# Eleven gate blocks placed anew in a hybrid DeltaNet and linear attention layer: one at the end of the linear attention, six in the delta rule, four behind it

## The chip, the cores and the metric

The kernel runs on one core of one Trainium2 chip. The metric is device microseconds of one execution. All numbers are in float32; matrix products that need the accuracy are made of three passes on TensorE with operands split into a high and a low part (type fp32r).

## The reference

One layer over a sequence of 1024 tokens of width 1024. What matters here are the two merge gates: two column groups of the one input projection, whose sigmoids weigh the two branches.

```python
h = rmsnorm(x, norm_mix_g[i])
proj = h @ w_in[i]
(gq, gk_, gv, gz, ga, gb, lq, lk, lv, lr, lgate, gate_a, gate_b) = jnp.split(proj, split_at, axis=-1)
...
o_a = gated_delta_rule_chunked(q_a, k_a, v_a, ...)        # 8 heads of 128, chunked
o_a = rmsnorm(o_a, gdn_norm_g[i]) * silu(gz)
y_a = o_a @ w_branch_gdn[i]
...
o_b = gla_chunked(q_b, k_b, v_b, ...)                     # 4 heads, linear attention
o_b = rmsnorm(o_b, gla_norm_g[i]) * silu(lr)
y_b = o_b @ w_branch_gla[i]

merged = jax.nn.sigmoid(gate_a) * y_a + jax.nn.sigmoid(gate_b) * y_b
x = x + merged @ w_out[i]
# then cross attention over 256 memory tokens, a squared-relu MLP, a final norm
```

gate_a and gate_b are 1024 columns each. Together they are 16 blocks of 128 columns, and each block needs only h (the normed input) and its own weights. A block may be computed at any time between the norm of x and the merge. That freedom is what the change uses.

## The kernel before, in words

**Phases in order.** Folding of the cross attention's weights and the norm of x; gate blocks 0 to 3; linear attention (`phase_gla`, 4 heads h, gate block 4 among its first projection); delta rule (`phase_gdn`, 4 pairs p of heads); two gate blocks and the loading of the merge's operands (in `run`); merge (`phase_merge`), output projection, cross attention and MLP.

**A gate block** (`push_gate`) is a unit of dense work: weights of 512 KB are loaded and split (ScalarE copies the high part, VectorE or GpSimd subtracts for the low part), 2 halves of 24 matmuls of 512 columns each follow into one PSUM tile each, ScalarE takes the tanh of each half into an SBUF tile, and SP stores it to DRAM (`tgd[i]`). The merge later loads these 32 halves back. The normed h stands in four slots of SBUF (A0a, A0b, A1a, A1b); every gate block and every projection of the delta rule reads them.

**Dense units and fills.** `push` puts a unit into a queue as a generator; each step of it emits one matmul (a unit of 48 matmuls has 49 steps, since one is spent after its weights). `fill(n)` takes n steps from the front of the queue, `until(name)` runs the queue to the end of a named unit, `drain` empties it. The phases are written as short chains (scan, norm, substitution) with such calls between their parts, so that TensorE has matmuls to do while a chain waits on VectorE or ScalarE.

**The delta rule's pair.** Per pair the queue gets q (2 units), v (2), a gate block, the next pair's keys (2), another gate block, z (2). The chain is: keys of the first head; output of the pair before (`gdn_norm`, then, once the queue has been run to its z, `gdn_out` with transposes and L1379, then `gdn_sums`, which stores to `oad`); keys of the second head; substitution (`gdn_subst`: 31 steps of two VectorE operations, L1250 and L1252); queries and v; inverse (`gdn_inverse`); scan over 8 chunks (`gdn_scan`). The fills between them come from GF and NFILL: 24 + 24 + 16 between the v units and the inverse, 8 four times in the inverse, 4 at 22 places in the scan. Behind the last pair one more gate block is pushed, 12 steps are filled, the norm is issued, 20 more are filled, and the outputs follow.

**The linear attention's end.** The last head (h = 3) has the unit r3 (84 matmuls, gate of the output) as its only dense work. Its scan has no fills (FI = 0); then `gla_norm` (L1045 scales the output v), the rest of the queue, and `gla_out` (transposes of v, L582, and the products that are stored to `obd`).

**Behind the delta rule.** `run` opens the SBUF pools of the merge in the memory that the delta rule leaves, pushes gate blocks 14 and 15, issues the loads of the operands of merge passes 0 to 3 (`obd` through three staging tiles "e", then splits into the slots B0a, B0b, B1a, B1b), and drains. Only then are passes 4 to 6 loaded, into t4 (memory of the gate blocks' weights), A1a and A1b (memory of h). The first merge product makes 7 passes in that order, for two groups of columns at once, 12 matmuls each.

**What sets the order.** The Python order is not the order of issue. The program is traced once, a planner (`Plan`) simulates it with costs of its own, and its order for every engine is laid down in a second trace. TensorE takes the matmul that stands earliest in the trace among those that are ready; the other engines go by latest start times. Tiles of one tag keep their order. So a change of the trace changes the planned order everywhere, within what is ready and what buffers allow. DMAs are issued by SP in the planned order, each waiting at the head of the queue.

Few lines that the words don't say, from `phase_gla`:

```python
                self.until(f"r{h}")
                self.gla_norm(sp, v[h % 2], ss)
```

for the first three heads, and for the last

```python
                    self.gla_norm(sp, v[h % 2], ss)
                    self.drain()
                    self.gla_out(sp, h, v[h % 2], sr)
```

Of the kernel before, what the change touches and what calls it, by code (L numbers as in the profile page):

```python
# [18 lines left out]
P = 128  # L19
D = 1024  # L20
T = 1024
NB = 8
MEM = 256
GH = 8
LH = 4
XH = 4
EPS = 1e-6
HALF = 512
# [13 lines left out]
XO = (('K3', 'Q1', 'V0'), ('V0', 'V1', 'O2'))  # L42
LOVU = (5,)
LOV = (0, 2, 5)


def c3(t):
# [393 lines left out]
class Layer:  # L441
# [624 lines left out]
    def phase_gla(self):  # L1066
        nc, a = self.nc, self.a
        with ExitStack() as ctx:
            sp = self.pool(ctx, "pgla", "right", bufs=2)
            self.bs[3] = self.late_h(self.t1d, lambda: self.ext(sp))  # L1070
            sm = self.sm = self.til(sp, [P, T], "sm", bufs=1)
            for tag, shape in (("qk", [P, T]), ("v", [P, NB, 256])):
                self.til(sp, shape, tag, bufs=2)
            self.pad(sp, 64)
            g4 = self.ext(sp)

            def done(i, half):
                if i == 1:
                    x = g4[:, half * HALF:(half + 1) * HALF]
                    nc.scalar.activation(x, x, AF.Tanh, scale=0.5)  # L1080
                    nc.sync.dma_start(self.tgd[4][:, half * HALF:(half + 1) * HALF], x)

            qk, ev = self.gla_qk(sp)
            self.push("u0", self.gla_dense([self.into(lambda i, half: (sm, g4)[i][:, half * HALF:(half + 1) * HALF],
                                                      1.0, done), ev]))
            self.until("u0")
            v = self.push_gla_v(sp, 0)
            self.fill(FA)
            bc = self.gla_gate(sp, 0)
            gb = self.decay_rows(sp)  # L1090
            prep = self.gla_prep(sp, qk, bc)
            self.until("v0")
            self.decay_cols(gb)
            sr = self.push_gla_r(sp, 0)
            self.fill(FB)
            for h in range(LH):
                AT, kdt = self.gla_scores(sp, *prep[:3], qk[1])
                self.fill(FC)
                ss = self.gla_scan(sp, AT, kdt, qk[0], v[h % 2], prep[3], FH if h < LH - 1 else FI)
                if h == LH - 1:  # L1100
# [3 lines that stand above are left out]
                    break  # L1104
                self.until(f"r{h}")
                self.gla_norm(sp, v[h % 2], ss)
                bc = self.gla_gate(sp, h + 1)
                qk, ev = self.gla_qk(sp)
                self.push(f"qk{h + 1}", self.gla_dense([ev]))
                self.fill(FD)  # L1110
                self.gla_out(sp, h, v[h % 2], sr)
                self.until(f"qk{h + 1}")
                prep = self.gla_prep(sp, qk, bc)
                if h == 1:
                    v = self.push_gla_v(sp, 2)
                    self.until("v2")
                    self.fill(FB)
                after = None
                if h == LH - 2:
                    def after(p):  # L1120
                        if p == 3:
                            self.hb[0, 1] = self.late_h(self.b12d, lambda: self.til(self.wp, [P, T], "raw", bufs=RAWS))
                sr = self.push_gla_r(sp, h + 1, after)
                self.fill(FG if h == 1 else FE)


# [266 lines left out]
        for q, x in enumerate((b11, b21, T2, T1, T3, b22, T4)):  # L1393
            nc.sync.dma_start(self.oad[q][:, p], x)

    def push_gate(self, i, getw, sp, tag="tg", tbufs=3):

        nc = self.nc

        def evict(half, pt):  # L1400
            t = self.til(sp, [P, HALF], tag, bufs=tbufs)
            nc.scalar.activation(t, pt, AF.Tanh, scale=0.5)
            nc.sync.dma_start(self.tgd[i][:, half * HALF:(half + 1) * HALF], t)

        self.push(f"g{i}", self.g_fm(lambda: getw(self.a["w_gate"][i]), evict))

    def phase_gdn(self, wp):

        nc, a = self.nc, self.a
        with ExitStack() as ctx:  # L1410
            sp = self.pool(ctx, "pgdn", "right", bufs=2)
            sq = self.pool(ctx, "pgdn2", "right", bufs=2)
            self.subPT = self.til(sp, [P, 16, P], "subPT", bufs=1)
            nc.gpsimd.memset(self.subPT, 0.0)
            self.pad(sp, 224, ([P, T], "k", 4), ([P, T], "dm", 2), ([P, T], "q", 2), ([P, T + 64], "cin", 2), ([P, T], "kdt", 2),
                     ([P, T], "NT", 2), ([P, T], "Pm", 1), ([P, 256], "pr", 1), ([P, 16, P], "PF", 1))

            for tag in ("v", "X", "acc", "AT"):
                self.til(sq, [P, T], tag, bufs=2)
            self.pad(sq, 96, ([P, HALF], "tg", 3))  # L1420

            def push_keys(hs):
                sts = [{}, {}]
                for h, st in zip(hs, sts):
                    st["k"] = self.til(sp, [P, NB, P], "k", bufs=4)
                    self.push_conv(wp, sp, sq, f"k{h}", GH + h, a["w_gdn"][4 * h], lambda acc, st=st: st["k"])
                return sts

            gates = iter(range(5, 14))
            getw = lambda src: self.wunit(wp, src)  # L1430
            last = None
            sts = push_keys((0, 1))
            for st, h in zip(sts, (0, 1)):
                self.gdn_decay(sp, sq, h, st)
            for p in range(GH // 2):
                hs = (2 * p, 2 * p + 1)
                for h, st in zip(hs, sts):
                    st["q"] = self.til(sp, [P, NB, P], "q", bufs=2)
                    self.push_conv(wp, sp, sq, f"q{h}", h, a["w_gdn"][4 * h + 1], lambda acc, st=st: st["q"])
                for h, st in zip(hs, sts):  # L1440
                    def out(acc, st=st):
                        st["vT"] = c3(acc)
                        return st["vT"]
                    self.push_conv(wp, sp, sq, f"v{h}", 2 * GH + h, a["w_gdn"][4 * h + 2], out)
                self.push_gate(next(gates), getw, sq)
                nxt = None
                if p < GH // 2 - 1:
                    nxt = push_keys((2 * p + 2, 2 * p + 3))
                self.push_gate(next(gates), getw, sq)
                for h, st in zip(hs, sts):  # L1450
                    self.push_gdn_z(wp, sp, sq, h, st)
                self.until(f"k{hs[1]}")
                self.fill(GF[0])
                if last:
                    for h, st in last:
                        self.gdn_norm(sq, st)
                self.gdn_keys(sp, sq, hs[0], sts[0])
                self.fill(GF[1])
                if last:
                    self.until(f"z{last[1][0]}")  # L1460
                    for h, st in last:
                        self.gdn_out(h, st)
                        self.fill(GF[2])
                    self.gdn_sums(p - 1, [st for _, st in last])
                self.gdn_keys(sp, sq, hs[1], sts[1])
                PF = self.gdn_subst(sp, sq, sts)
                self.until(f"v{hs[0]}")
                self.gdn_queries(sp, sq, sts[0])
                self.fill(GF[3])
                self.gdn_queries(sp, sq, sts[1])  # L1470
                self.until(f"v{hs[1]}")
                self.gdn_v(sq, sts[0])
                self.fill(GF[4])
                self.gdn_v(sq, sts[1])
                self.fill(GF[5])
                self.gdn_inverse(sts, PF, GF[6])
                if nxt:
                    for st, h in zip(nxt, (2 * p + 2, 2 * p + 3)):
                        self.gdn_decay(sp, sq, h, st)
                self.gdn_scan(sq, hs, sts, NFILL)  # L1480
                last, sts = list(zip(hs, sts)), nxt
            self.push_gate(next(gates), getw, sq)
            self.fill(12)
            for h, st in last:
                self.gdn_norm(sq, st)
            self.until(f"z{last[1][0]}")
            self.fill(20)
            for h, st in last:
                self.gdn_out(h, st)
            self.gdn_sums(3, [st for _, st in last])  # L1490
            self.drain()
# [691 lines left out]
    def run(self):  # L2183
# [41 lines left out]
        with ExitStack() as ctx:  # L2225
# [2 lines left out]
            sp = self.pool(self.ctx, "plate", "right")  # L2228
            self.pad(sp, 32, ([P, HALF], "e", 3), ([P, HALF], "acc", 2), ([P, HALF], "q", 4))
            self.bp2 = self.pool(self.ctx, "big2", "right")  # L2230
            for i in (14, 15):
                self.push_gate(i, lambda src: self.wunit(wp, src), sp, "acc", 2)
            self.wp = self.pool(self.ctx, "w4", "right")
            self.queue_w()
# [114 lines left out]
```

## Time and profile before

| | |
|---|---|
| median of 3 runs | 2225.49 us (2225.03 to 2226.25) |
| the profiled execution, its time | 2225.38 us |
| its span, first to last instruction | 2223.4 us |
| mean granted TensorE clock | 0.990 |
| linear attention ends, delta rule's first matmuls | some 506 us |
| substitutions of the four pairs start | 562.6, 711.1, 864.7, 1018.2 us |
| first merge pass starts | 1151.4 us |

Lines of the profile name a line of the kernel (L1250), an engine (PE TensorE, PEld its weight loads, DVE VectorE, ACT ScalarE, POOL GpSimd, SPq the issue of DMAs by SyncE) and tiles as written and read (wlo<-raw,whi). In the view of stretches a row holds the start and end, the length, for each engine its busy time and in brackets its instructions, the granted clock, the share of the DMA engines' time, and GB/s. In the view of waits a row reads: engine, tile and line, the releaser, then total us, times, longest. A few matmul records are missing from a trace.

### The profile page before, as it was taken

How to read it: one execution, taken by the hardware profiler on the slowest of the kernel's cores; microseconds unless marked ns; L12 is line 12 of the kernel's file. 1: busy time of each engine (PE TensorE's matmuls, PEld its weight loads, DVE VectorE, ACT ScalarE, POOL GpSimd, SP SyncE). 2: the span in 40 equal slices, each digit the busy share in tenths (PEclk: the TensorE clock that was granted, in tenths of full speed). 3: DMA queues.
4: the chain of work that ended last, by engine and by line, in shares of the span. 5: the costliest groups of instructions: out<-in, count | busy, mean ns of one | idle time of the engine just before them, and what ended most of it. 6: DMA issues, size and time to landing. Idle time of an engine off the chain costs nothing.

```text
span 2223.4 us, 32153 instructions
## 1 busy us (share of the span) xinstructions
PE 2163.1 (97%) x11552; PEld 1851.5 (83%) x11552; DVE 1658.8 (75%) x3016; ACT 1100.1 (49%) x2223; POOL 187.5 (8%) x218
## 2 busy tenths in 40 slices
PE   7899999999999999999999999999999999999996
PEld 7788988878898888888877888998888888888886
DVE  7835999797966957759558994559998778667756
ACT  6443655354554545445534443455665556544433
POOL 2100111002111111111000000000100000000011
PEclk8999999999999999999999999999999999999998
DMA  6852111213212212121177771235364446778742
GB/s 233 280 175 83 58 66 47 71 62 100 72 34 77 62 39 91 39 81 43 57 250 231 259 246 57 98 126 158 121 199 146 157 156 197 253 246 282 244 122 81
DMA packets 148463, 300.20 MB, mean 135 GB/s; under 512 B 15816, under 2 KB 22344, under 8 KB 148304
## 3 DMA queue, kind: packets, MB, share of 16 engines
q1 hardware_dynamic: 141504, 289.75, 40.0%
q10 hardware_dynamic: 6800, 8.42, 1.1%
q8 instruction: 90, 1.47, 0.3%
q14 instruction: 69, 0.57, 0.1%
HBM read 212.35 MB, written 85.75 MB: 134 GB/s over the span
## 4 chain that ended last, share of the span: by engine, by line
PE 63%; DVE 11%; ACT 1%; issue 1%; DMA 1%; POOL 0%; DVEq 0%; ACTq 0%; POOLq 0%
PE pd L512 14%; PE pd L514 14%; PE pd L510 14%; PE ps L512 5%; PE ps L514 5%; PE ps L510 5%; DVE acc L1146 2%; DVE Pm L1252 1%; DVE pr L1250 1%; PE ps L1285 1%; PE ps L582 1%; PE ps L1325 1%; PE ps L1342 1%; PE ps L1205 1%; PE ps L1332 1%
## 5 line engine op out<-in xcount | busy, mean ns | idle before, releaser
L550 ACT ACTIVATE wop<-raw 128x512 fp32r<-128x512 f32 (+1 forms) x444 | 297.2, 675 | 497.4 <-PE pd L514 225.4
L551 DVE TENSOR_TENSOR wop<-raw,wop 128x512 fp32r<-128x512 f32 (+1 forms) x402 | 288.7, 721 | 142.8 <-ACT wop L550 135.5
L550 ACT ACTIVATE whi<-raw 128x512 fp32r<-128x512 f32 x86 | 52.1, 625 | 99.2 <-PE pd L512 65.0
L1146 DVE SCALAR_TENSOR_TENSOR acc<-cin,convw,acc 128x1024 f32<-128x1024 f32 x72 | 92.4, 1284 | 2.6 <-ACT acc L1144 2.3
L510 PE MATMUL pd<-t,wop 128*128 128x512 f32 x220 | 86.7, 394 | 2.4 <-ACT t L550 2.4
L514 PE MATMUL pd<-t,wop 128*128 128x512 f32 x220 | 89.0, 404 | 0.0
L512 PE MATMUL pd<-t,wop 128*128 128x512 f32 x220 | 86.4, 393 | 0.2 <-DVE t L551 0.2
L510 PE MATMUL pd<-B1a,wop 128*128 128x512 f32 (+1 forms) x220 | 82.8, 376 | 0.0
L514 PE MATMUL pd<-B1a,wop 128*128 128x512 f32 (+1 forms) x220 | 82.5, 375 | 0.0
L551 DVE TENSOR_TENSOR wlo<-raw,whi 128x512 fp32r<-128x512 f32 x77 | 52.0, 688 | 36.1 <-ACT whi L550 34.0
L510 PE MATMUL pd<-A0a,whi 128*128 128x512 f32 x172 | 69.7, 405 | 0.0
L510 PE MATMUL pd<-A1b,whi 128*128 128x512 f32 x172 | 69.1, 401 | 0.0
L512 PE MATMUL pd<-A1a,whi 128*128 128x512 f32 x172 | 68.2, 397 | 0.0
L514 PE MATMUL pd<-A1b,wlo 128*128 128x512 f32 x172 | 68.0, 395 | 0.0
L512 PE MATMUL pd<-A1b,whi 128*128 128x512 f32 x172 | 68.0, 395 | 0.0
L514 PE MATMUL pd<-A1a,wlo 128*128 128x512 f32 x172 | 67.9, 395 | 0.0
L512 PE MATMUL pd<-A0b,whi 128*128 128x512 f32 x172 | 67.9, 394 | 0.0
L514 PE MATMUL pd<-A0a,wlo 128*128 128x512 f32 x172 | 67.8, 394 | 0.0
L510 PE MATMUL pd<-A1a,whi 128*128 128x512 f32 x172 | 67.6, 393 | 0.0
L512 PE MATMUL pd<-B0b,wop 128*128 128x512 f32 x172 | 67.2, 391 | 0.2 <-DVE B0b L551 0.2
L510 PE MATMUL pd<-A0b,whi 128*128 128x512 f32 x172 | 67.3, 391 | 0.0
L512 PE MATMUL pd<-A0a,whi 128*128 128x512 f32 x172 | 67.3, 391 | 0.0
(598 smaller groups left out, 6971.6 us busy)
## 6 DMA issues: line engine op xcount, KB each, us to landing
raw<-in_w_dram SPq DMA_DIRECT2D x120, 256.0 KB, 3.7
raw<-in_w_gdn_dram SPq DMA_DIRECT2D x64, 256.0 KB, 2.9
raw<-in_w_dram SPq DMA_DIRECT2D x32, 512.0 KB, 3.8
e<-ad SPq DMA_DIRECT2D x63, 256.0 KB, 4.5
ad<-q SPq DMA_DIRECT2D x45, 256.0 KB, 2.9
rawa<-ad SPq DMA_DIRECT2D x42, 256.0 KB, 5.0
A0b<-tgd SPq DMA_DIRECT2D x32, 256.0 KB, 5.3
ad<-acc SPq DMA_DIRECT2D x30, 256.0 KB, 2.4
```

Of the source, the lines that this page charges most:

```text
L510: nc.tensor.matmul(out, lh, rh, start=first and i == 0, stop=False)
L512: nc.tensor.matmul(out, lh, rl, start=False, stop=False)
L514: nc.tensor.matmul(out, ll, rh, start=False, stop=last and i == n - 1)
L550: nc.scalar.activation(hi, raw, AF.Copy)
L551: (lo_eng or nc.gpsimd).tensor_tensor(lo, raw, hi.bitcast(F32), SUB)
L582: self.nc.tensor.transpose(pt[:, i * P:(i + 1) * P], s, self.ident)
L1146: nc.vector.scalar_tensor_tensor(acc, cin[:, 1 + i:1 + i + T], cw[:, i:i + 1], acc, MUL, ADD)
L1205: nc.tensor.matmul(pt[:, i * P:(i + 1) * P], kc, kc, start=True, stop=True)
L1250: nc.vector.tensor_tensor(pr, X[:, c + 1:32, c:c + 1].broadcast_to([P, m, n]), Pm[:, c:c + 1, 0:n].broadcast_to([P, m, n]), MUL)
L1252: nc.vector.tensor_tensor(Pm[:, c + 1:32, 0:n], Pm[:, c + 1:32, 0:n], pr, ADD)
L1285: nc.tensor.matmul(pt[0:96, i * n:(i + 1) * n], PF[:, v + i, 0:96], Z, start=True, stop=True)
L1325: nc.tensor.matmul(py[:, 0:P], st["NT"][:, c, :], zh[h], start=True, stop=True)
```

## The change

GP and GLG are new constants. One gate block (block 5) is pushed behind r3 in the linear attention, with weights through that phase's ring and results in tiles of its tag "ex". In the delta rule only the first pair pushes a block ahead of the next keys; all four pairs keep the block behind them, and one more follows the last pair: blocks 6 to 11. Blocks 12 to 15 are pushed where 14 and 15 were. The number of blocks, their matmuls and stores stay the same.

```diff
+GP, GLG = 1, 1
...
                 sr = self.push_gla_r(sp, h + 1, after)
+                if h == LH - 2:
+                    for i in range(5, 5 + GLG):
+                        self.push_gate(i, lambda src: self.wpart(src, [NB, P], nc.vector), sp, "ex", EXB, T)
                 self.fill(FG if h == 1 else FE)
...
-    def push_gate(self, i, getw, sp, tag="tg", tbufs=3):
+    def push_gate(self, i, getw, sp, tag="tg", tbufs=3, width=HALF):
...
-            t = self.til(sp, [P, HALF], tag, bufs=tbufs)
+            t = self.til(sp, [P, width], tag, bufs=tbufs)[:, :HALF]
...
-            gates = iter(range(5, 14))
+            gates = iter(range(5 + GLG, 16))
...
-                self.push_gate(next(gates), getw, sq)
+                if p < GP:
+                    self.push_gate(next(gates), getw, sq)
                 nxt = None
                 if p < GH // 2 - 1:
                     nxt = push_keys((2 * p + 2, 2 * p + 3))
...
-            for i in (14, 15):
+            for i in range(10 + GLG + GP, 16):
                 self.push_gate(i, lambda src: self.wunit(wp, src), sp, "acc", 2)
```

## The prediction

> **What bounds the kernel now.** I read the page first (busy time and the 40 slices), then the TensorE waits, then busy time in chosen stretches.
>
> ```profile
> span 2223.4 us, 32153 instructions
> PE 2163.1 (97%) x11552; PEld 1851.5 (83%) x11552; DVE 1658.8 (75%) x3016; ACT 1100.1 (49%) x2223; POOL 187.5 (8%) x218
> PE   7899999999999999999999999999999999999996
> DVE  7835999797966957759558994559998778667756
> ```
>
> TensorE is busy 97% of the span. The gate blocks are 16 before and after, so no TensorE work is saved: time can only come from places where TensorE stands still or is slowed. A busy share hides some of that, because a matmul's end is modelled; counting matmuls shows it better. A full stretch of 512-column matmuls is the 1200 row below: 223 in 50 us, 0.225 us each.
>
> ```profile
> 497.50:502.50 5.00, 0.35 (x3) 0.03 (x1) 3.45 (x9) 2.12 (x5) 1.64 (x1) 0.99 0.00 0
> 502.50:506.00 3.50, 3.50 (x17) 3.50 (x18) 2.40 (x3) 0.00 (x0) 0.00 (x0) 0.53 0.20 76
> 1121.30:1123.00 1.70, 1.70 (x18) 1.66 (x16) 1.03 (x2) 0.00 (x0) 0.00 (x0) 1.00 0.00 0
> 1162.50:1172.50 10.00, 7.32 (x24) 5.06 (x22) 7.25 (x13) 3.52 (x7) 0.00 (x0) 0.83 0.84 280
> 1172.50:1181.10 8.60, 6.47 (x26) 4.20 (x24) 6.20 (x11) 4.50 (x9) 0.00 (x0) 1.00 0.74 238
> 1181.10:1188.60 7.50, 4.91 (x14) 3.39 (x13) 4.78 (x8) 3.50 (x6) 0.00 (x0) 0.77 0.67 229
> 1200.00:1250.00 50.00, 50.00 (x223) 41.40 (x222) 48.32 (x81) 26.94 (x48) 0.00 (x0) 1.00 0.72 239
> ...
> PE ps L582 <- DVE v L1045: 4.7, 1, 4.7
> PE pd L512 <- DVE B1a L551: 2.5, 1, 2.5
> PE pd L510 <- ACT t L550: 2.4, 1, 2.4
> PE ps L510 <- ACT B1b L550: 1.3, 1, 1.3
> ```
>
> The columns of the stretches are length, then TensorE, its weight loads, VectorE, ScalarE, GpSimd (busy, instructions), granted clock, DMA share, GB/s. Two places behind the kernel's start lose time. **Place A** is the end of the linear attention (497.5 to 506.0): a wait of 4.7 us for the normed output (v, L1045), then transposes at a clock of 0.53. The two rows hold 20 matmuls, 16 of them transposes. Transposes of the same kind fill the row 1121.3 to 1123.0 (16 and a little more in 1.70 us), so the 20 are worth 1.7 + 4 x 0.225 = 2.6 us, and 8.5 - 2.6 = 5.9 us are lost. **Place B** is the first merge pass, 1162.5 to 1188.6: 24 + 26 + 14 = 64 matmuls in 26.1 us, worth 64 x 0.225 = 14.4 us, so 11.7 us are lost, on operand tiles loaded back from DRAM (B1a, B1b, t). In both places the clock falls right behind a wait. The change touches both, and takes TensorE work out of the delta rule between them.
>
> The Trainium skill, "TensorE: Matmul & The Clock Gate", Part 1, says the array drops to half clock after an idle window of about 3.4 us. By it the waits of 2.5 and 2.4 us in place B would cost only themselves. Here the trace differs: the rows behind them show 0.83 over 10 us and 0.77 over 7.5 us, that is 1.7 us each.
>
> **Part 1: block 5 behind r3.** Its 48 matmuls follow r3's last ones and stand ahead of the transposes that wait. How long a block is:
>
> ```profile
> L1402 ACT ACTIVATE acc<-pd x4: 598/598/599, 1135.3 to 1151.7; 128x512 f32<-128x512 f32 x4
> L1402 ACTq EVENT_SEMAPHORE  x9: 17/17/5227, 594.7 to 1146.4; - x9
> ...
> 479.28 1.22 DVE L551 TENSOR_TENSOR A1b<-raw,A1b 128x1024 fp32r<-128x1024 f32 x1
> 479.97 1.05 ACT L550 ACTIVATE A1b<-raw 128x1024 fp32r<-128x1024 f32 x1
> 482.87 0.81 SPq L479 DMA_DIRECT2D raw<-in_w_gdn_dram  x2
> ...
> 497.42 0.40 PE L514 MATMUL pd<-t,wop 128*128 128x512 f32 x1
> 502.47 1.75 PE L582 MATMUL ps<-ident,v 128*128 128x128 f32 x7 [4.65 <-DVE v L1045]
> ...
> L1403 SPq DMA_DIRECT2D tgd<-tg x26: 319/327/432, 143.4 to 1131.3; - x26
> DMA to landing us min/median/max: 2.0/3.9/8.9
> ```
>
> Blocks 14 and 15 evict four halves in 1135.3 to 1151.7: 16.4 / 3 = 5.5 us a half, 10.9 us a block (48 x 0.225 = 10.8). The wait is 4.65 us from 497.8, so 10.8 us cover it twice, and with no standstill the half clock goes too. Up to 5.9 us are won. What the block adds there: one load of 512 KB, one split of 1.05 us on ScalarE and 1.22 us on VectorE, two tanh of 0.6 us, two stores. The load goes onto SP's queue near the delta rule's first weights, which before the change are issued at 482.87, long before their first matmul (behind the transposes from 502.47). The split shares VectorE with the norm that is waited for: at most 1.2 us later, under the block's cover. If that cover were not there (operands late), the wait is back and nothing is won; if the first conv's buffers then also wait for the two stores to land, 3.9 us are lost. Bounds -3.9 to +5.9; I take +5.4, near the upper end, because the cover is twice the wait.
>
> **Part 2: the delta rule without three blocks.** The first head pair keeps two blocks, pairs 1 to 3 lose one each: 10.8 us of TensorE work less per period. Does anything else set the period?
>
> ```profile
> L1250 DVE TENSOR_TENSOR pr<-X,Pm x29: 192/354/426, 711.1 to 756.0; 128x31 f32<-128x31 f32 x2, 128x60 f32<-128x60 f32 x2, 128x87 f32<-128x87 f32 x2, 128x112 f32<-128x112 f32 x2
> L1250 DVE TENSOR_TENSOR pr<-X,Pm x29: 193/355/424, 864.7 to 909.7; 128x31 f32<-128x31 f32 x2, 128x60 f32<-128x60 f32 x2, 128x87 f32<-128x87 f32 x2, 128x112 f32<-128x112 f32 x2
> ...
> 711.10:756.50 45.40, 45.40 (x234) 38.57 (x233) 44.35 (x97) 21.49 (x60) 6.18 (x9) 1.00 0.25 77
> 756.50:777.60 21.10, 20.76 (x166) 18.53 (x164) 17.10 (x23) 12.76 (x20) 3.96 (x8) 1.00 0.09 26
> 777.60:806.10 28.50, 28.50 (x204) 25.79 (x204) 18.70 (x53) 18.68 (x71) 2.33 (x3) 1.00 0.06 20
> 806.10:864.70 58.60, 58.60 (x288) 49.37 (x287) 32.33 (x76) 25.50 (x65) 11.40 (x15) 1.00 0.24 81
> ...
> L1372 DVE TENSOR_TENSOR v<-v,rs_o x2: 1221/1222/1224, 810.1 to 815.3; 128x1024 f32<-128x1024 f32 x2
> L1379 DVE SCALAR_TENSOR_TENSOR X<-ps,ghalf,X x4: 743/747/751, 835.6 to 841.2; 128x512 f32<-128x512 f32 x4
> ```
>
> The period is 864.7 - 711.1 = 153.6 us. Its stretches are substitution (45.4; VectorE 98% busy), inverse (21.1), scan (28.5) and the rest up to the next substitution (58.6). The fills are counts: 64 matmuls between the v units and the inverse, 32 in it, 88 in the scan. These find other units in place of the lost block (the next keys), so the first three stretches keep their TensorE work. What shrinks is the last one, where the queue is run up to z. It is serial only in parts: norm from 806.1 to 815.3 + 1.2 = 816.5 (10.4 us), and from the first output row at 835.6 to the next substitution at 864.7 (29.1 us). Together 39.5 us, against 58.6 - 10.8 = 47.8 us of TensorE work that stay: 8.3 us to spare. So a period gets shorter by the whole block. Pair 3 is tighter: behind its v units are three units (147 steps) where 184 are asked for, so 37 matmuls (8.3 us) are missing from the end of its scan. The planner lets TensorE take any later ready matmul, and block 11 (48) is ready then. I take -1.0 us for all of this, bounds 0 and -8.3 (nothing pulled ahead). If next keys' convs enter VectorE's full 45 us, they wait; keys are due only at the scan's end.
>
> **Part 3: two more blocks behind the delta rule** (12 to 15 for 14 and 15).
>
> ```profile
> 1107.71 1.28 SPq L479 DMA_DIRECT2D e<-obd  x3
> 1132.55 0.32 SPq L479 DMA_DIRECT2D e<-obd  x1
> 1145.50 1.92 SPq L479 DMA_DIRECT2D A0a<-in_xT_dram  x4
> 1157.91 0.96 SPq L479 DMA_DIRECT2D rawa<-obd  x2
> ...
> 1151.43 0.39 PE L510 MATMUL pd<-B0a,wop 128*128 128x512 f32 x1
> 1183.78 0.50 PE L510 MATMUL pd<-t,wop 128*128 128x512 f32 x1 [2.38 <-ACT t L550]
> ...
> 1151.40:1162.50 11.10, 11.10 (x50) 9.20 (x49) 4.76 (x8) 4.50 (x8) 0.00 (x0) 1.00 1.03 374
> ```
>
> Loads for the merge's operands start when the delta rule's memory is free (1132.55) and the merge starts at 1151.43, with 19 us of lead. Two blocks more make the lead 21.6 us longer, less up to 8.3 us that the last scan takes ahead: at least 13.3 us, against 11.7 us of lateness. That covers passes 0 to 3. Pass 4 (t) and 5, 6 (A1a, A1b) fill memory that the gate blocks use until their last matmul, so their lead does not grow. But t is wanted only 8 x 12 x 0.225 = 21.6 us behind the merge's start, and its first raw loads go out 6.5 us behind it (1157.91). DMA went to 374 GB/s in the row shown, so the rate has room. The blocks put four more weight loads and four stores on SP's queue among the operand loads, and a store waits for its tanh. The longest hold in ScalarE's queue ahead of a block's tanh was 5.2 us (above), and operand splits behind such a tanh would wait with it. All that lies in the new 13 us or more. Bounds 0 and +11.7; I take +9.7, leaving 2.0 us for a wait before t.
>
> **Sum.** 5.4 - 1.0 + 9.7 = 14.1 us. The profiled execution took 2225.38 us (span 2223.4), 0.1 below the median of 2225.49; 2225.4 - 14.1 = 2211.3, so 2211 us, 0.6% faster. A measurement of this kernel tells a difference from 0.2%, 4.5 us.
>
> **Rivals.**
> (1) Slower: the delta rule's serial chain sets the period, not TensorE. Then TensorE idles in the place of each block taken out. For it: VectorE's 98% in the substitution, and 8.3 us of spare is small. Against: the 58.6 us stretch has no wait. If nothing is saved in pairs 1 to 3, 32.4 us of blocks are added elsewhere: 2225.4 + 32.4 - 5.4 - 9.7 = 2242.7 us. It decides from 15.1 us of idle time, 5.0 us in each period. At 7 us each it gives 2225.4 - 15.1 + 21 = 2231 us. By the clock rows above, each wait of some 2.5 us would cost 1.7 us more; by the skill's rule under 3.4 us it would not.
> (2) The lateness moves to t, whose memory is freed by the last block. If t keeps its distance from the merge's start (1183.78 - 1151.43 = 32.4 us against 21.6 us wanted), 10.8 us are still lost and part 3 is worth 0.9: 2225.4 - 5.4 + 1.0 - 0.9 = 2220 us. Against: before, t's loads stood behind the late ones of passes 2 and 3.
> (3) Block 5 does not cover place A (weights late, or the planner orders it away): 2211.3 + 5.4 = 2217 us.
> (4) Nothing: the planner's new order loses elsewhere what is won; 2225 us.
>
> **How the numbers follow.** Forecast 0.60, rival 1 0.09, rival 2 0.14, rival 3 0.07, rival 4 0.10. Forecast, 2 and 3 are faster by over 0.2% (0.81), rival 4 is the same (0.10), rival 1 slower (0.09). The forecast's own range is 2204 to 2217: 5.9 + 11.7 = 17.6 us won gives 2207.8, and the planner's reordering may take a few waits more or less. The range goes up to 2221 to hold rivals 2 and 3.
>
> **What would show it.** Right: the wait for v (L1045) is gone or under 1 us; the clock stays at 1.00 there and in the first merge pass; waits for B1a and B1b are gone; the substitutions of pairs 2 and 3 start 143 us apart; 222 matmuls in each 50 us there. Wrong: TensorE waits of several us in the delta rule, on VectorE's Pm, zh or X; a wait before t longer than 2.4 us; a tanh on ScalarE that holds up operand splits.

## The result, and the profile after

The changed kernel takes 2208.15 us (median of 4 runs, 2207.26 to 2209.57) against 2225.87 us before (median of 4). The ratio is 0.9917, 95% interval 0.9906 to 0.9929: 17.7 us less. The profiled execution took 2207.92 us, its span is 2206.2 us. Lines behind the edit stand 1 to 5 lines further down than before (L512 is L513, L1045 is L1046, L1250 is L1254).

The page of the changed kernel, in the lines that answer to those of before:

```profile
span 2206.2 us, 32145 instructions
PE 2155.9 (98%) x11552; PEld 1848.5 (84%) x11552; DVE 1658.0 (75%) x3012; ACT 1103.6 (50%) x2222; POOL 200.9 (9%) x221
```

The number of matmuls is the same, and VectorE is as busy as before; the span is shorter by 17.2 us. Stretches of the changed kernel (length, then each engine's busy time and instructions, clock, DMA): the end of the linear attention with the same 8.5 us length, the first 50 us of the merge, and the substitutions of pairs 1 and 2. Behind them, of the kernel before, the first 50 us of the merge, then places A and B each as one stretch (a matmul on the border of two rows is counted in both, so the 20 and 64 of the prediction's rows are 19 and 60 here):

```profile
500.00:508.50 8.50, 8.50 (x39) 7.01 (x38) 5.55 (x12) 3.31 (x9) 1.64 (x1) 1.00 0.00 0
1148.30:1198.30 50.00, 50.00 (x222) 41.40 (x221) 40.39 (x66) 22.37 (x40) 0.00 (x0) 1.00 0.82 274
719.70:773.40 53.70, 53.70 (x271) 45.43 (x271) 53.04 (x106) 26.07 (x68) 6.30 (x10) 1.00 0.22 66
862.00:915.60 53.60, 53.60 (x270) 45.39 (x269) 52.95 (x106) 26.07 (x68) 6.29 (x10) 1.00 0.21 66
```

```profile
1151.40:1201.40 50.00, 42.59 (x165) 32.36 (x164) 34.73 (x57) 21.27 (x37) 0.00 (x0) 0.93 0.81 273
497.50:506.00 8.50, 3.85 (x19) 3.53 (x18) 5.85 (x11) 2.12 (x5) 1.64 (x1) 0.80 0.08 31
1162.50:1188.60 26.10, 18.70 (x60) 12.64 (x59) 18.22 (x30) 11.52 (x20) 0.00 (x0) 0.87 0.76 251
```

At place A TensorE now runs 39 matmuls in 8.5 us where it ran 19, at full clock. At place B the first 50 us of the merge hold 222 matmuls, the full rate, where they held 165: (222 - 165) x 0.225 = 12.8 us that are no longer lost. The TensorE waits around place A in the changed kernel (engine, tile and line, releaser, total, times, longest):

```profile
PE ps L1025 <- DVE S L1029: 1.1, 1, 1.1
PE ps L1000 <- DVE ex L978: 1.0, 1, 1.0
PE ps L583 <- DVE qk L982: 0.4, 1, 0.4
```

The wait of 4.7 us for v is gone; a new one of 1.1 us has come, for the scan's first state S (see the pinned split below). Why place B is covered shows in the order of TensorE: the last transposes of the delta rule's output, then gate blocks, then the merge.

```profile
1100.96 1.03 PE L583 MATMUL ps<-ident,v 128*128 128x128 f32 x8
1101.75 0.47 PE L515 MATMUL pd<-A1a,wlo 128*128 128x512 f32 x1
```

From 1102.0, when these transposes end, to the merge's start at 1148.3 there are 46 us; before, 28.4 us (1123.0 to 1151.4). The lead grew by 18 us.

Where the time was won can be read from two stretches that hold the same number of matmuls in both kernels: from the norm of the third head of the linear attention, up to which TensorE's order is the same in all runs, to the merge's first matmul, and from there to the end. The kernel before, then the changed one:

```profile
441.20:1151.40 710.20, 702.78 (x3986) 604.04 (x3985) 524.59 (x1113) 360.20 (x941) 103.35 (x146) 1.00 0.22 71
1151.40:2223.40 1072.00, 1045.39 (x5053) 881.30 (x5051) 803.75 (x1377) 522.51 (x935) 41.07 (x30) 0.99 0.55 181
```

```profile
443.60:1148.30 704.70, 700.21 (x3986) 601.21 (x3985) 529.29 (x1118) 366.72 (x949) 112.08 (x149) 1.00 0.23 76
1148.30:2206.20 1057.90, 1039.59 (x5053) 879.83 (x5051) 796.93 (x1368) 518.80 (x926) 45.79 (x30) 0.99 0.55 180
```

Place A and the delta rule together are 5.5 us shorter, the rest 14.1 us. The stretch ahead happened to take 2.4 us longer in this execution (443.6 against 441.2), which is why the spans differ by 17.2 and not by 19.6 us.

### The profile page after: what moved, and what is told of

Same layout as the page of the kernel before. It is cut to its first block, busy times and chain, and to the rows that moved or that the text cites. A ratio compares the mean times of both kernels' runs of the same rounds, so it can differ in the third digit from the quotient of the medians.

```text
span 2206.2 us, 32145 instructions
## 1 busy us (share of the span) xinstructions
PE 2155.9 (98%) x11552; PEld 1848.5 (84%) x11552; DVE 1658.0 (75%) x3012; ACT 1103.6 (50%) x2222; POOL 200.9 (9%) x221
## 4 chain that ended last, share of the span: by engine, by line
PE 77%; DVE 15%; issue 4%; ACT 2%; DMA 2%; POOL 0%; DVEq 0%; ACTq 0%; SPq 0%; POOLq 0%
PE pd L515 18%; PE pd L511 18%; PE pd L513 18%; PE ps L513 5%; PE ps L511 5%; PE ps L515 5%; DVE acc L1150 2%; PE ps L1289 1%; PE ps L583 1%; DVE Pm L1256 1%; DVE pr L1254 1%; DVE wop L552 1%; DVE wlo L552 1%; PE ps L1329 1%; DMA rawa<-hd 1%
## 5 line engine op out<-in xcount | busy, mean ns | idle before, releaser
L513 PE MATMUL pd<-t,wop 128*128 128x512 f32 x220 | 85.7, 390 | 0.0
L513 PE MATMUL pd<-B0b,wop 128*128 128x512 f32 x172 | 67.2, 391 | 0.2 <-DVE B0b L552 0.2
L515 PE MATMUL pd<-A1a,wop 128*128 128x512 f32 x168 | 67.0, 399 | 0.0
L513 PE MATMUL pd<-A1b,whi 128*128 128x512 f32 x168 | 66.8, 398 | 0.0
L515 PE MATMUL pd<-A0b,wlo 128*128 128x512 f32 x168 | 66.3, 395 | 0.0
L513 PE MATMUL pd<-A1a,whi 128*128 128x512 f32 x168 | 66.3, 395 | 0.0
L513 PE MATMUL pd<-A0a,whi 128*128 128x512 f32 x168 | 66.2, 394 | 0.0
L511 PE MATMUL pd<-A0b,whi 128*128 128x512 f32 x168 | 66.2, 394 | 0.0
```

The source lines that it names most:

```text
L511: nc.tensor.matmul(out, lh, rh, start=first and i == 0, stop=False)
L513: nc.tensor.matmul(out, lh, rl, start=False, stop=False)
L515: nc.tensor.matmul(out, ll, rh, start=False, stop=last and i == n - 1)
```

## The experiments

Edits are shown against the changed kernel. Each run is compared with executions of the kernel before that were taken together with it; a ratio stands with its 95% interval.

**Block 5 alone.**

```diff
-GP, GLG = 1, 1
+GP, GLG = 3, 1
```

> Block 5 alone is moved to the end of the linear attention; pairs 1 and 2 of the delta rule keep two blocks, pair 3 keeps one, 14 and 15 stay behind. Theory (the waits add up): place A loses about 5 us less, place B keeps its 12 to 13 us; 2225.9 - 5 = 2221 us. Rival (the gain comes from the planner's new order or a shorter delta rule): within 1.5 us of before, or over 10 us faster.

Measured: 2217.77 us, ratio 0.9961 (0.9947 to 0.9976), 8.7 us faster (5.3 to 11.8) than the 2226.91 of before; more than the 5 expected, in between the theory and its rival. The stretches and the waits of the merge:

```profile
1145.90:1195.90 50.00, 44.34 (x190) 34.81 (x189) 38.49 (x63) 22.31 (x38) 0.00 (x0) 1.00 0.78 267
496.50:505.00 8.50, 8.50 (x39) 7.07 (x38) 5.62 (x12) 3.46 (x10) 1.64 (x1) 1.00 0.00 0
```

```profile
PE ps L511 <- ACT B1b L551: 3.1, 2, 1.8
PE pd L513 <- DVE B1a L552: 2.2, 1, 2.2
```

Place A is as in the change (39 matmuls). Place B still waits for B1a and B1b, but loses 32 x 0.225 = 7.2 us instead of 12.8: no single wait is over 2.2 us, the clock stays at 1.00, and t does not wait; later some 4 us are lost that before were not (short waits for B0a and B0b, below, among them). From the merge's first matmul to the end this run takes 1070.5 us against 1072.0, so place B keeps nearly its whole loss, as the theory said; the stretch ahead of it is 4.9 us shorter. These 6.4 us of one execution lie inside the interval of the 8.7. Why t's wait went with this plan was not tried.

**Two blocks behind the delta rule, none at the linear attention.**

```diff
-GP, GLG = 1, 1
+GP, GLG = 2, 0
```

> Two blocks more behind the delta rule (12 to 15), taken from pairs 2 and 3; block 5 stays in the delta rule. Theory (the waits add up): place A keeps its wait of 4.7 us and its half clock, place B is free of waits; 2225.9 - 12.9 = 2213 us, and with the run of block 5 alone the two gains sum to the change's 17.7. Rival (the two parts need each other): 2217 us or more.

Measured: 2214.81 us, ratio 0.9938 (0.9925 to 0.9951), 13.8 us by the ratio. The theory holds for the two places: the trace shows no TensorE wait at all between 1120 and 1210, the merge's first 50 us hold 222 matmuls, and place A waits as before:

```profile
1154.80:1204.80 50.00, 50.00 (x222) 41.41 (x221) 40.39 (x66) 22.34 (x40) 0.00 (x0) 1.00 0.82 279
```

```profile
PE ps L583 <- DVE v L1046: 4.6, 1, 4.6
```

By the medians the gains of this run and of block 5 alone sum to 8.7 + 13.8 = 22.5 us and not to the 17.7 that were expected. The wide intervals of both allow it; by the two stretches of the traces (table below) they sum to 18.3 us, against 19.6 of the change and 18.2 of its repeat, so the parts add up as far as that can tell.

**One block behind the delta rule.**

```diff
-GP, GLG = 1, 1
+GP, GLG = 3, 0
```

> One block more behind the delta rule (13 to 15), taken from pair 3. Theory (lead against lateness): the lead grows by 10.8 us less what the last scan takes ahead, so of 12.9 us lost some 3 to 6 stay, as waits for B1b or t; 2216 to 2219 us. Rival (the waits are set by when the memory is freed by the last block): place B keeps over 10 us; 2224 us. Rival (any block there is enough): 2213 us.

Measured: 2218.00 us, ratio 0.9955 (0.9942 to 0.9968). Lead against lateness holds in size, though the wait that is left is for A1a and not for B1b or t:

```profile
1153.10:1203.10 50.00, 48.05 (x209) 38.56 (x208) 38.87 (x63) 23.22 (x41) 0.00 (x0) 1.00 0.79 283
```

```profile
PE ps L513 <- DVE A1a L552: 2.0, 2, 1.1
```

No block more loses 12.8 us there, one block 13 x 0.225 = 2.9, two none. The wait that is left is for A1a, memory of h that the last gate block frees. The prediction held that the lead cannot move this part, but with two blocks the wait is gone; what set it here was not traced.

**No block left in pairs 1 to 3.** Their second block goes too; seven blocks (9 to 15) stand behind the delta rule.

```diff
-GP, GLG = 1, 1
+GP, GLG, GS = 1, 1, 1
...
-                self.push_gate(next(gates), getw, sq)
+                if p < GS:
+                    self.push_gate(next(gates), getw, sq)
                 for h, st in zip(hs, sts):
                     self.push_gdn_z(wp, sp, sq, h, st)
...
-            for i in range(10 + GLG + GP, 16):
+            for i in range(6 + GLG + GP + GS, 16):
```

> As the change, but pairs 1 to 3 lose their second block too; 9 to 15 stand behind the delta rule. Theory (the serial chain is near): in the changed kernel the stretch from scan's end to the next substitution is down to 42 to 44 us against 39.5 serial, so each period gives back only 2 to 5 us of the 10.8 and TensorE waits 6 to 8 us a period on VectorE; 2208 + 15 to 24 = 2223 to 2232 us. Rival (TensorE still sets the period, since the substitution can shrink from 53.6 back to 45.4): 2208 to 2213 us.

Measured: 2212.58 us, ratio 0.9933 (0.9919 to 0.9947). The rival is right in its time and in that TensorE still sets the period, and the theory of a near serial chain fell; but the substitution did not shrink back to 45.4 us as the rival had it (52.0 us in pair 2). What shrank is the stretch behind the scan. The rows: the substitution of pair 2; the stretch from the third scan's end to the last substitution; the stretch behind that substitution; TensorE's waits in the delta rule.

```profile
853.50:905.50 52.00, 52.00 (x263) 44.05 (x262) 50.86 (x104) 26.57 (x69) 6.81 (x12) 1.00 0.20 61
949.40:984.70 35.30, 35.30 (x191) 30.19 (x190) 30.39 (x72) 21.41 (x62) 12.13 (x15) 1.00 0.25 83
1024.10:1046.60 22.50, 19.97 (x151) 18.67 (x150) 14.08 (x24) 10.21 (x16) 1.18 (x4) 0.85 0.08 24
```

```profile
PE ps L1280 <- ACT PF L1266: 3.6, 4, 2.5
PE ps L583 <- DVE acc L1156: 0.7, 1, 0.7
```

The stretch that I had put at 39.5 us of serial work took 35.3 us with TensorE busy throughout. What idles is another place: the last pair's inverse waits 2.5 us for PF, the substitution's result, and the clock falls behind it (0.85 over 22.5 us, 3.4 us worth). Up to the merge this run takes 6.0 us more than the change. The longer waits (3.6 against 1.4 us for PF, 0.7 against 0.4 for acc) and the 3.4 us of clock are 5.9 of them. So with three blocks less pairs 1 to 3 still keep TensorE busy, and the first limit is the last pair's inverse.

**Five blocks behind: the first pair loses one as well.**

```diff
-GP, GLG = 1, 1
+GP, GLG = 0, 1
```

> As the change, but the first pair loses its block ahead of the keys too: five blocks behind the delta rule (11 to 15). Theory (a block is worth only the wait that it covers): the merge has no wait left, so 10.8 us more of lead win nothing, and the first period shrinks by the block: 2208 us, within 2 us of the change. Rival (more lead helps the later passes as well): 2204 us or less. Rival (the first pair needs the block, since its convs fill VectorE): 2211 us or more, with waits behind the first substitution.

Measured: 2205.83 us, ratio 0.9908 (0.9895 to 0.9921). Its interval overlaps the change's 0.9917 (0.9906 to 0.9929): once the waits are covered, more cover wins nothing that can be told.

**Place A with r3's own matmuls.** All gate blocks in their old places (GP = 4, GLG = 0 gives the kernel before), with one fill changed:

```diff
-GP, GLG = 1, 1
+GP, GLG = 4, 0
...
-                self.fill(FG if h == 1 else FE)
+                self.fill(FG if h == 1 else FE if h == 0 else 24)
```

> The kernel before, all blocks in their old places; only the fill behind r3's push is 24 instead of 48 steps in the last round, so 24 more of r3's own matmuls stand behind the last scan. Theory (place A needs any 4.7 us of ready matmuls, not a gate block): 24 x 0.225 = 5.4 us cover the wait and the half clock; 2225.9 - 5 = 2221 us, if nothing is missed where the 24 were. Rival (they are needed where they stood, ahead of the scores, or the planner takes them into the scan): the wait for v stays or a new one ahead of the scores takes its place; 2224 to 2229 us.

Measured: 2230.68 us, ratio 1.0016 (1.0007 to 1.0024), 3.6 us slower, and slower than either expectation. The wait for v did shrink to 1.9 us, so other ready matmuls cover it too; but two waits came, one of them larger than what was won (TensorE's waits around place A, then its first matmul of the delta rule, SP's issue of its first weights and the wait of the store ahead of that issue; last, the issue in the kernel before, and the wait in SP's queue ahead of it):

```profile
PE pd L511 <- ACT whi L551: 5.8, 1, 5.8
PE ps L583 <- DVE v L1046: 1.9, 1, 1.9
PE pd L511 <- ACT ex L868: 1.6, 1, 1.6
...
507.92 0.80 PE L511 MATMUL pd<-A0a,whi 128*128 128x512 f32 x1 [5.79 <-ACT whi L551]
...
502.68 0.89 SPq L480 DMA_DIRECT2D raw<-in_w_gdn_dram  x2
...
SPq L1561 <- DVE ex L1056: 26.1, 2, 25.4
```

```profile
482.87 0.81 SPq L479 DMA_DIRECT2D raw<-in_w_gdn_dram  x2
...
SPq L479 <- PE pd L514: 5.4, 1, 5.4
```

The delta rule's first weights are loaded 20 us later. Before, they were issued as soon as a matmul of r3 was done, since their tiles lie over the memory of the operands of the linear attention (t), which r3 reads. Here the last matmuls of r3 on t end at 498.0, and the load then still stood behind an output store at the head of SP's queue, which waited 25.4 us for the last head's output. So the queue's order ended the wait; that the moved matmuls are why the planner placed the load there is argued. A gate block reads only the four slots of h, which stay in use anyway. That this property, and not just 10.8 us of work, makes block 5 the better cover fits both runs; the memory alone was not tried.

**The split of block 5's weights left free.**

```diff
-self.push_gate(i, lambda src: self.wpart(src, [NB, P], nc.vector), sp, "ex", EXB, T)
+self.push_gate(i, lambda src: self.wpart(src, [NB, P]), sp, "ex", EXB, T)
```

> As the change, but the subtraction that splits block 5's weights may go to GpSimd instead of being fixed to VectorE. Theory (the new wait of 1.1 us for the scan's first state S is VectorE splitting block 5's weights ahead of it): it goes back to 0.3 us; 2208.2 - 1 = 2207 us. Rival (that wait has another source, or GpSimd's slower subtraction delays block 5): 2208 to 2210 us.

Measured: 2207.77 us, ratio 0.9917 (0.9904 to 0.9929). The edit changed nothing: the argument is only a starting point for a sum that the planner places, and all five engines have the same instructions in the same order as in the change. So it is a repeat of the change, and as such it agrees with it (the wait for S is 1.1 us again); it says nothing on the cause of that wait.

**A split pinned to VectorE.** In `late_h` the subtraction is called on the engine itself, past the planner's choice.

```diff
-            self.split(raw, t[:, 0, i:i + 2], t[:, 1, i:i + 2], self.nc.vector)
+            self.split(raw, t[:, 0, i:i + 2], t[:, 1, i:i + 2], self.tc.nc.vector)
```

> As the change, but the late split of A1b in the linear attention is pinned to VectorE (the planner had put one of its two subtractions on GpSimd, where it ran 2.9 us beside VectorE's split of block 5's weights, which took 2.8 us instead of 1.2). Theory (the two sums slow each other, and the scan's first state S stands behind): block 5's split takes 1.2 us again, the wait for S goes from 1.1 to at most 0.4 us; 2207 us, within 1.5 us of the change. Rival (that split is long for another reason, such as a wait for its ScalarE part): 2.8 us again, S waits 1.1 us or more.

Measured: 2205.71 us, ratio 0.9897 (0.9882 to 0.9911). The changed kernel first, then this one (start, length, operation):

```profile
487.51 2.81 DVE L552 TENSOR_TENSOR wop<-raw,wop 128x1024 fp32r<-128x1024 f32 x1
490.25 0.68 DVE L935 SCALAR_TENSOR_TENSOR ex<-th,ex 128x512 f32<-128x512 f32 x1
490.85 0.68 DVE L861 TENSOR_TENSOR ex<-pd,ex 128x512 f32<-128x512 f32 x1
491.45 0.41 DVE L1029 COPY S<-ps 128x256 f32<-128x256 f32 x1
...
486.34 2.90 POOL L552 TENSOR_TENSOR A1b<-raw,A1b 128x1024 fp32r<-128x1024 f32 x1
```

```profile
488.10 0.41 DVE L1029 COPY S<-ps 128x256 f32<-128x256 f32 x1
488.43 0.67 DVE L861 TENSOR_TENSOR ex<-pd,ex 128x512 f32<-128x512 f32 x1
489.03 1.21 DVE L552 TENSOR_TENSOR wop<-raw,wop 128x1024 fp32r<-128x1024 f32 x1
```

With no subtraction on GpSimd beside it, block 5's split takes 1.21 us instead of 2.81, and the wait for S is gone from the list of TensorE's waits. The pin also moved the copy of S ahead of the split, so the two effects are not taken apart. Against the change the whole times do not tell a gain, since the two intervals overlap. The stretch up to the merge does: 703.0 us against 704.7 in the change and 704.6 in its repeat, one execution each.

**Both: five blocks behind and the pinned split.**

```diff
-GP, GLG = 1, 1
+GP, GLG = 0, 1
...
-            self.split(raw, t[:, 0, i:i + 2], t[:, 1, i:i + 2], self.nc.vector)
+            self.split(raw, t[:, 0, i:i + 2], t[:, 1, i:i + 2], self.tc.nc.vector)
```

> Five blocks behind the delta rule (none ahead of the keys in any pair), and the split pinned as in the run before. Theory (each wait that is covered counts for itself): 2205 us, the time of the five-block run less up to 1. Rival (the planner's new order costs more than the wait): 2207 to 2210 us.

Measured: 2206.12 us, ratio 0.9897 (0.9880 to 0.9914), against the same runs of before as the pinned split alone. Nothing that can be told is won on top of it. The pinned split with the change's own placing is as good as any version here; what it wins over the change, some 1.7 us up to the merge, is too small for the whole times to show.

**The two stretches in every run.** Us in the profiled execution, from the norm of the third head to the merge's first matmul, and from there to the end of the span. Each run has the same matmuls in both.

| run | to the merge | behind |
|---|---|---|
| before | 710.2 | 1072.0 |
| the change | 704.7 | 1057.9 |
| its repeat (split left free) | 704.6 | 1059.4 |
| block 5 alone | 705.3 | 1070.5 |
| two blocks behind, none at A | 710.3 | 1060.0 |
| one block behind, none at A | 711.5 | 1063.4 |
| seven blocks behind | 710.7 | 1061.5 |
| five blocks behind | 704.3 | 1058.5 |
| r3's own matmuls | 715.1 | 1073.2 |
| pinned split | 703.0 | 1059.1 |
| five blocks behind, pinned split | 703.2 | 1058.6 |

The change and its repeat differ by 0.1 us in the first column and by 1.5 in the second; smaller differences than that say nothing.

## Why the prediction was right

The forecast was 2211 us with 14.1 us won, the result 2208.15 with 17.7. The number did not come from errors that cancel: both parts of the sum came out above their forecast. The sum's terms, one by one:

**Place A (+5.4 forecast).** The mechanism held: wait and half clock both went. The 19 matmuls of 8.5 us (the prediction counted 20, with the one on the border of its rows twice) became 39. The new wait of 1.1 us for S, on VectorE behind the split of block 5's weights, was foreseen as a delay of the norm by at most 1.2 us under cover; it came at the scan instead, where nothing covered it. The stretch that holds place A and the delta rule is 5.5 us shorter (5.6 in the repeat, 4.9 with block 5 alone). That is the 5.4 of this term; with the -1.0 of the next the forecast for the two was 4.4.

**The delta rule (-1.0 forecast).** The substitutions of pairs 1 and 2 start at 719.7 and 862.0, 142.3 us apart, where 142.8 follow from a whole block saved. Where two blocks were taken out and place A was left alone, the stretch is as long as before (710.3 against 710.2 us; 711.5 with one block taken out), so the delta rule gave the blocks back, within some 1 us. But the inside went another way than the prediction's step. The step "so the first three stretches keep their TensorE work" is wrong for the substitution, which now holds 271 matmuls instead of 234, and "If next keys' convs enter VectorE's full 45 us, they wait" is wrong too: they entered and did not wait. VectorE's operations on the line that sums the convs, within the substitution, before and after:

```profile
711.10:756.50 45.40, 11.53 (x9) 1.00 0.25 77
```

```profile
719.70:773.40 53.70, 19.22 (x15) 1.00 0.22 66
```

Fifteen of these operations instead of nine take 7.7 us more, and the substitution grew from 45.4 to 53.7 us. It cost nothing, since the stretch behind the scan shrank by more than one block, from 58.6 to 41.1 us:

```profile
820.90:862.00 41.10, 41.10 (x209) 34.77 (x208) 28.34 (x71) 21.37 (x57) 12.73 (x16) 1.00 0.26 84
```

The "8.3 us to spare" were too few: the 39.5 us are no floor, since the run without blocks in pairs 1 to 3 did that stretch in 35.3.

**Place B (+9.7 forecast).** The lead grew by 18 us, within the 13.3 to 21.6 forecast. (The prediction's rows show three loads already at 1107.71; the fourth, at 1132.55, goes out 18.9 us ahead of the merge. In the change the fourth goes out at 1114.87, and this distance grew by 14.6 us, to 33.5.)

```profile
1114.87 1.00 SPq L480 DMA_DIRECT2D e<-obd  x2
```

The term was sized too low, in two ways. The loss was 12.6 to 12.8 us and not 11.7: the three rows summed to 64 matmuls because those on their borders were counted twice, and as one stretch they hold 60, worth 13.5 of the 26.1 us. And the 2.0 us left for a wait before t did not come. With one block moved 2.9 us stay, with two none. From the merge's start to the end 14.1 us were won (12.6 in the repeat).

**The rivals.** Rival 1 (the serial chain sets the period) would need 5 us of idle time in each period; in all four together TensorE waits 1.8 us (1.4 for PF, 0.4 for acc), and the run with three blocks less again lost only some 4 us to the change. Rival 2 (the wait moves to t) did not come. That t's loads were held up by those of passes 2 and 3 and not by their memory is argued; the run of block 5 alone has no wait for t either, with no more blocks behind the delta rule than before. Rival 3 is excluded by the 39 matmuls, rival 4 by the interval.

**The clock.** By the rule of the Trainium skill, "TensorE: Matmul & The Clock Gate", Part 1, of an idle window of about 3.4 us, the waits of 2.5 and 2.4 us would not have cost clock. The run without blocks in pairs 1 to 3 shows the same as the kernel before: 0.85 over 22.5 us behind a wait of 2.5 us, and later 0.83 over 10 us (1576 to 1586) with two waits of 1.1 and 0.8 us. In the run of block 5 alone a wait of 2.2 us (B1a) was not followed by half clock, but two short ones later in the merge were (waits, then the stretch):

```profile
PE pd L513 <- DVE B0b L552: 1.2, 1, 1.2
PE pd L511 <- ACT B0a L551: 0.4, 1, 0.4
```

```profile
1309.00:1316.50 7.50, 5.83 (x18) 4.07 (x17) 7.50 (x13) 1.86 (x3) 0.00 (x0) 0.77 0.54 171
```

The measurement decides: waits far below 3.4 us, alone or two close together, were followed by half clock here, and not each of them. No threshold follows from so few.

## What to carry to other kernels

Count matmuls in a stretch against the full rate, not busy time, and count each place as one stretch: the two places lost some 6 and 12.8 us in a kernel whose TensorE is 97% busy. Independent work is worth what it covers, and no more: one block behind the delta rule won ten of the 12.8 us, the second the rest, the third nothing. To size the parts of a change, compare stretches between two instructions that both kernels have, with the same matmuls in between: the whole times move by microseconds for reasons that lie ahead of the edit. Before filling a gap with work taken from elsewhere, ask what memory that work holds and what it moves in the DMA queue: r3's own matmuls covered part of the same wait and made the kernel slower, because the next phase's weights were loaded 20 us later.

## What the runs showed of the hardware that was not expected

A subtraction of 128x1024 on VectorE took 2.81 us while GpSimd ran one of the same size (2.90 us), against 1.21 us alone. The Trainium skill, "GPSIMD Engine Reference", section 1 (Specifications), says that GpSimd's SBUF interfaces are shared with VectorE, with contention from VectorE instructions with two SBUF inputs; the trace agrees, with a factor of 2.3 for this pair. VectorE's ended 1.08 us behind GpSimd's (490.32 against 489.24), close to the 1.21 us that it needs alone, as if it had got little done beside the other; the repeat of the change has the same two durations. Not every such overlap costs: a subtraction of 128x512 that VectorE had started 0.03 us ahead of GpSimd's took 0.68 us, as this size does elsewhere.

```profile
486.31 0.68 DVE L552 TENSOR_TENSOR wop<-raw,wop 128x512 fp32r<-128x512 f32 x1
```
